# The weight sums of the Strassen groups as accumulating DMAs, each group in two items

## The chip, the cores and the metric

One core of one Trainium2 chip runs the kernel. The metric is the time of one execution in microseconds (us) on the device. Two runs of the kernel before took 727.15 and 727.75 us, median 727.45.

The engines are named as in the profile: PE (TensorE's matmuls), PEld (its weight loads), DVE (VectorE), ACT (ScalarE), POOL (GpSimd) and SP (SyncE, which here only issues DMAs).

## What is computed

One decoder layer on 256 tokens of width 1024 in float32: a SwiGLU feed-forward part, a mixing part (a state-space branch and a differential-attention branch, merged by gates), and a second SwiGLU feed-forward part, each between two RMS norms and with a residual. The edited code stands in the two feed-forward parts:

```python
def swiglu(x, w_gate, w_up, w_down):
    return (jax.nn.silu(x @ w_gate) * (x @ w_up)) @ w_down
...
h = h + 0.5 * rmsnorm(swiglu(rmsnorm(h, ffn1_pre_g[l]), ffn1_w_gate[l], ffn1_w_up[l], ffn1_w_down[l]),
                      ffn1_post_g[l])
...
h = h + 0.5 * rmsnorm(swiglu(rmsnorm(h, ffn2_pre_g[l]), ffn2_w_gate[l], ffn2_w_up[l], ffn2_w_down[l]),
                      ffn2_post_g[l])
```

`w_down` is 2816 x 1024: 11 row blocks of 256.

## The kernel before

**Weights.** All weights come through one list, `chunks`, of 1 MB pieces in the order of use. SP loads them (L164) into raw tiles `raw<i>`: three buffers with the tag "raw", and for a few chunks (`IN_U8`) one of two buffers with the tag "u8" that the normed activations leave free meanwhile. `load_next` issues the next load when a chunk's last reader has been written down; on the chip, the load waits until its buffer is free.

**Splits.** PE multiplies in float32r. Each operand is split into a high part, a cast on ACT (L258), and the rest, a subtraction on DVE (L259); a product is made of three matmuls (high x high, low x high, high x low). A split of half a chunk, 128 x 1024 elements, is one *step*: one cast, one subtraction, two tiles from the pool of 28 "k4" buffers. `split_to` writes steps down some way ahead of the product that needs them (`AHEAD`, `STEPS`). ACT, DVE, PE and SP execute in the order written; POOL's order is left to the framework's scheduler. A step therefore waits for its raw tile, for the step before it on ACT and DVE, and for PE to have finished with the k4 buffers that it reuses.

**The down projection.** `mm_n` (L489) multiplies the 256 tokens (two blocks of 128) with the row blocks of `w_down`, in the order of the table `DOWNS`. A plain row block (`0`, `1`, ...) is one chunk: two steps and 24 matmuls of 128 x 512. A pair such as `(2, 3)` is a *group*: its 512 rows, its 256 tokens and its 1024 columns are halved, and the 2 x 2 x 2 block product is done in 7 products instead of 8, the Strassen-Winograd form. `quarters` (L655) forms and splits the activations' quarters and their sums; `piece_steps` (L191) those of the weights. The weights of a group are two chunks, whose column halves are named b11 and b12 (first chunk) and b21 and b22 (second). Their sums are formed in place, by four subtractions on DVE (L209) between the seven splits; `piece` (L520) issues the seven products, 6 matmuls each. Three of them gather in PSUM tiles of their own over all groups of a part (`acc_m`: m5, m6, m7) and one in m1; after the last group `sums_of` and `sum_up` (L529, L535) add them to the four accumulators `acc_f`.

In the first part two groups, in the second three, all of them among plain blocks. The last `TAIL` (3; in the second part 2) plain blocks are multiplied at the end, one accumulator after the other, so that the norm behind them (`post_norm`) starts early. The gain row of that norm, `pg_f`, is loaded by POOL (L486).

Of the kernel before, what the change touches and what calls it, by code (L numbers as in the profile page):

```python
# [24 lines left out]
P = 128  # L25
T = 256
# [17 lines left out]
DOWNS = (((2, 3), 0, (4, 5), 1, 6, 7, 8, 9, 10), ((2, 3), 0, (4, 5), 1, 8, (6, 7), 9, 10))  # L44
# [7 lines left out]
def tile_hybrid_layer(ctx: ExitStack, tc: tile.TileContext, x, ffn1_pre_g, ffn1_w_gate, ffn1_w_up,  # L52
# [37 lines left out]
    chunks, pieces, in_u8 = [], set(), set()  # L90

    def t_chunk(w, k0, c0):
        chunks.append((w[k0:k0 + D, c0:c0 + T].rearrange("(j p) c -> p j c", p=P), [P, KD, T]))

    def s_chunk(w, k0, c0):
        chunks.append((w[k0:k0 + 512, c0:c0 + 512].rearrange("(j p) c -> p j c", p=P), [P, 4, 512]))

    def n_chunk(w, k0):
        chunks.append((w[k0:k0 + 2 * P, :].rearrange("(j p) c -> p j c", p=P), [P, 2, D]))

    w_in2 = w_in[0]
    Z0, XS0, B0, C0, DT0, Q0, KK0, V0, G0 = 0, 2048, 4096, 4608, 5120, 5152, 6176, 7200, 8224

    def ffn_chunks(wg, wu, wd, downs, first=False):
# [5 lines left out]
        n = 0  # L110
        for item in downs:
            if isinstance(item, tuple):
                pieces.add(len(chunks))
                n += 1
                in_u8.update(len(chunks) + m for m in range(2) if (not first, n, m) in IN_U8)
            for j in item if isinstance(item, tuple) else (item,):
                n_chunk(wd[0], j * T)
# [30 lines left out]
    def load_next(i):  # L148
        n = i + 1 + RAW_BUFS
        while n - len(in_u8.intersection(range(i + 1, n))) < i + 1 + RAW_BUFS:  # L150
            n += 1
        load_to(n)

    def load_to(n, at={}):
        while len(raws) < min(n, len(chunks)):
            i = len(raws)
            src, shape = chunks[i]
            if i in in_u8:
                r = sb.tile(shape, F32, tag="u8", name=f"raw{i}", bufs=2)
            else:  # L160
                r = sb.tile(shape, F32, tag="raw", name=f"raw{i}", bufs=RAW_BUFS)
# [6 lines left out]
    def split_steps(ahead=True):  # L168


        i = len(splits)
        load_to(i + 1)
# [4 lines left out]
        for q in range(2):  # L177
# [5 lines left out]
            for j in range(0, nj, n):  # L183
                js = slice(j, j + n)
                f = split(hi[:, js, :], lo[:, js, :], r[:, q * nj + j:q * nj + j + n, :])
                if i in behind:
                    tc.add_manual_dep(f.ins, behind[i], order, reason="behind the sums")
                if (q, j + n) == (1, nj):
                    raws[i] = r = None
                    if ahead:  # L190
                        load_next(i)  # L191
                yield

    def piece_steps():


        i = len(splits)
        load_to(i + 2)
        (b11, b12), (b21, b22) = ([r[:, :, q * 512:(q + 1) * 512] for q in range(2)] for r in raws[i:i + 2])
        pairs = []  # L200
        splits.extend((pairs, None))
        sums = {0: (b11, b12, b11), 1: (b12, b22, b12), 4: (b22, b22, b11), 5: (b21, b21, b22)}
        for n, out in enumerate((b11, b21, b22, b11, b12, b22, b21)):
            hi = k4([P, 2, 512], f"shi{i}{n}", F32R)
            lo = k4([P, 2, 512], f"slo{i}{n}", F32R)
            split(hi, lo, out)
            pairs.append((hi, lo))
            if n in sums:
                nc.vector.tensor_tensor(*sums[n], ALU.subtract)  # L209
            if n > 4:  # L210
                raws[i + n - 5] = None
                load_next(i + n - 5)
# [4 lines left out]
    def advance():  # L217

        while True:
            if under[0] is None:  # L220
                if len(splits) == len(chunks):
                    return False
                steps_at.extend([made_steps[0]] * (len(splits) + 1 - len(steps_at)))
                under[0] = piece_steps() if len(splits) in pieces else split_steps()
# [5 lines left out]
    def split_to(n, steps=0):  # L230

        while len(splits) < min(n, len(chunks)):
# [6 lines left out]
    def take(ahead=AHEAD):  # L239
# [6 lines left out]
        nj = chunks[i][1][1] // 2  # L246
        return (lambda j: his[j // nj][:, j % nj, :], lambda j: los[j // nj][:, j % nj, :])

    def take_part(n):
# [3 lines left out]
        if n == 6:  # L253
            taken[0] += 2
# [68 lines left out]
    halves = (slice(0, 512), slice(512, D))  # L323
# [165 lines left out]
    def mm_n(acc, acts, ready, turned, begun=lambda: None, items=(0, 1, 2, 3), tail=TAIL):  # L489
# [3 lines left out]
        held, sums = [], [None]  # L493
# [23 lines left out]
        def piece(c):  # L517
            outs = ((m1, 1), (acc[0][0], (0, 0)), (acc[0][1], (0, 1)), (m5, 5), (m7, 7), (m6, 6),
                    (acc[1][0], (1, 0)))
            for n, (out, key) in enumerate(outs):  # L520
                wh, wl = take_part(n)
                for kt in range(2):
                    ah, al = acts[c][n][kt]
                    for x_, w_ in ((ah, wh), (al, wh), (ah, wl)):
                        product(key, out, x_, w_[:, kt, :], kt == 1 and w_ is wl and c == inner[-1])
            del acts[c]

        def add(out, in_, x_):
            return nc.vector.tensor_tensor(out, in_, x_, ALU.add)  # L529

        def sums_of():
# [4 lines left out]
            for out, in_, x_, at in ((u2, m6, u1, None), (u4, m5, u2, (0, 1)), (u2, m7, u2, (1, 0)),  # L536
                                     (u3, m5, u2, (1, 1))):
                add(out, in_, x_)
# [3 lines left out]
        def sum_up(b, q):  # L542
            f = add(acc[b][q], acc[b][q], sums[0].pop((b, q)))
# [7 lines left out]
        for c in items[:-tail]:  # L551
            if isinstance(c, tuple):
                piece(c)
                if c == inner[-1]:
                    sums_of()
                continue
# [89 lines left out]
    def ffn(post_v, tag, products, ready, turned, then):  # L646
# [9 lines left out]
        def quarters(j0, j1):  # L656
# [15 lines left out]
            for n in range(2):  # L672
                split(fh[:, 2 * n:2 * n + 2], fl[:, 2 * n:2 * n + 2], f[n])
            acts[(j0, j1)] = [[(h_[:, n, k, :], l_[:, n, k, :]) for k in range(2)]
                              for h_, l_, n in ((ah, al, 0), (ah, al, 1), (fh, fl, 3), (fh, fl, 0), (fh, fl, 2),
                                                (fh, fl, 1), (ah, al, 2))]
# [68 lines left out]
    def first_products(evict, back):  # L745
# [33 lines left out]
        def ends(c):  # L779
            raws[c] = None  # L780
            load_to(c + 1 + RAW_BUFS)
# [679 lines left out]
```

## Time and profile before

| what | value |
|---|---|
| median of 2 runs | 727.45 us |
| the profiled execution | 727.35 us |
| its span in the trace | 725.6 us |
| granted clock of TensorE | 0.998 |
| DVE busy | 559.6 us, 77% of the span |
| ACT busy | 435.6 us, 60% |
| groups of the first part on PE | 130.3 to about 155 us |
| groups of the second part on PE | 663.7 to 673.2, 678.7 to 688.2, 699.1 to 708.6 us |

How to read it: the span runs from the first to the last instruction of the trace. A row of the list of groups has the line, the engine, the operation and the tiles (numbers left out), then the count, the busy time and the mean in ns, then the idle time of the engine before them and what ended it. A row of the chain has start, length and what ran. A row of the list of waits has the waiting instruction, the one waited for, the total in us, how often, and the longest. "raw<-raw" at L209 are the in-place sums of weights; "shi" and "slo" the split tiles of a group, "whi" and "wlo" those of a plain chunk.

### The profile page before, as it was taken

The page shows a single profiled execution, that of the slowest core. Times are in us where ns is not written, and L with a number is a line of the kernel's source. Part 1 is how long each engine was busy: PE and PEld are TensorE (multiplying, and loading weights), DVE is VectorE, ACT ScalarE, POOL GpSimd, SP SyncE. Part 2 cuts the span into 40 slices and gives each one's busy share as a digit, 9 for nine tenths or more (in the row PEclk, how much of TensorE's full clock was granted, in tenths as well). Part 3 has the DMA queues.
Part 4 walks back from the last instruction along what each step waited for, and adds up shares of the span by engine and source line. Part 5 has one row for each costly group of instructions (what it writes and reads, how often), then busy time and mean ns, then how long its engine had stood idle before and what let it go on. Part 6 is the DMA issues. An engine that isn't in the chain of part 4 may idle for free.

```text
span 725.6 us, 12188 instructions
## 1 busy us (share of the span) xinstructions
PE 716.9 (99%) x4917; PEld 652.9 (90%) x4917; DVE 559.6 (77%) x814; ACT 435.6 (60%) x703; POOL 34.7 (5%) x74
## 2 busy tenths in 40 slices
PE   8999999999999999999999999999999999999996
PEld 7899999888889999999998888888888999999885
DVE  5858769897668889876978988696684875578985
ACT  6735535665557565977966465974563645456642
POOL 0800000000300000000000000000010000000000
PEclk9999999999999999999999999999999999999999
DMA  8976364758453558565656655375361755765611
GB/s 320 286 221 220 129 232 146 289 175 285 128 174 117 188 164 272 166 205 189 216 163 190 210 192 175 116 244 191 118 230 60 231 184 168 231 231 193 227 76 58
DMA packets 94216, 138.03 MB, mean 190 GB/s; under 512 B 2684, under 2 KB 68304, under 8 KB 94160
## 3 DMA queue, kind: packets, MB, share of 16 engines
q1 hardware_dynamic: 91488, 129.51, 53.7%
q0 software_dynamic: 2368, 7.22, 3.3%
q8 instruction: 38, 0.62, 0.3%
q10 hardware_dynamic: 304, 0.53, 0.2%
q14 instruction: 18, 0.15, 0.1%
HBM read 136.17 MB, written 1.08 MB: 189 GB/s over the span
## 4 chain that ended last, share of the span: by engine, by line
PE 98%; ACT 1%; DMA 1%; DVE 0%; issue 0%; DVEq 0%; SPq 0%
PE acc_f L498 12%; PE pgt L283 6%; PE pws L283 6%; PE pg_f L268 5%; PE pg_f L269 5%; PE pup_f L269 4%; PE pup_f L268 4%; PE pup_f L271 4%; PE pg_f L271 4%; PE acc_m L498 4%; PE pn_f L776 3%; PE pn_mx L283 3%; PE pn_f L283 3%; PE acc_mx L498 3%; PE pwd L283 3%; PE pxs L268 2%
## 5 line engine op out<-in xcount | busy, mean ns | idle before, releaser
L259 DVE TENSOR_TENSOR wlo<-raw,whi 128x1024 fp32r<-128x1024 f32 (+1 forms) x226 | 265.8, 1211 | 27.3 <-ACT whi L258 23.5
L258 ACT CAST whi<-raw 128x1024 fp32r<-128x1024 f32 (+1 forms) x226 | 224.6, 1041 | 42.5 <-DMA raw<-in_ffn_w_up_dram 18.9
L269 PE MATMUL pg_f<-u_f,whi 128*128 128x256 f32 x288 | 67.1, 276 | 0.0
L269 PE MATMUL pup_f<-u_f,whi 128*128 128x256 f32 x288 | 67.1, 276 | 0.0
L268 PE MATMUL pg_f<-u_f,whi 128*128 128x256 f32 x288 | 67.1, 276 | 0.0
L268 PE MATMUL pup_f<-u_f,whi 128*128 128x256 f32 x288 | 67.0, 276 | 0.0
L268 PEld LDWEIGHTS pg_f<-u_f,whi 128*128 128x128 f32 x288 | 54.1, 188 | 0.0
L269 PEld LDWEIGHTS pup_f<-u_f,whi 128*128 128x128 f32 x288 | 54.1, 188 | 0.0
L268 PEld LDWEIGHTS pup_f<-u_f,whi 128*128 128x128 f32 x288 | 54.1, 188 | 0.0
L269 PEld LDWEIGHTS pg_f<-u_f,whi 128*128 128x128 f32 x288 | 54.0, 188 | 0.0
L258 ACT CAST shi<-raw 128x1024 fp32r<-128x1024 f32 x35 | 35.8, 1052 | 29.2 <-DVE raw L209 16.1
L259 DVE TENSOR_TENSOR slo<-raw,shi 128x1024 fp32r<-128x1024 f32 x35 | 42.1, 1219 | 2.2 <-PE acc_m L498 1.4
L271 PE MATMUL pup_f<-u_f,wlo 128*128 128x256 f32 x288 | 38.5, 276 | 0.0
L271 PE MATMUL pg_f<-u_f,wlo 128*128 128x256 f32 x288 | 38.5, 276 | 0.0
L721 DVE TENSOR_TENSOR sg_f<-pup_f,sg_f 128x512 f32<-128x512 f32 x18 | 12.4, 688 | 32.3 <-PE pup_f L271 32.3
L271 PEld LDWEIGHTS pg_f<-u_f,wlo 128*128 128x128 f32 x288 | 35.3, 188 | 0.0
L271 PEld LDWEIGHTS pup_f<-u_f,wlo 128*128 128x128 f32 x288 | 35.3, 188 | 0.0
L498 PE MATMUL acc_f<-whi,gh_f 128*128 128x512 f32 x96 | 33.5, 390 | 0.0
L498 PE MATMUL acc_f<-whi,gl_f 128*128 128x512 f32 x96 | 33.5, 389 | 0.0
L498 PE MATMUL acc_f<-wlo,gh_f 128*128 128x512 f32 x96 | 33.5, 389 | 0.0
L283 PE MATMUL pgt<-whi,u_mx 128*128 128x512 f32 x128 | 33.0, 394 | 0.0
L268 PE MATMUL pxs<-u_mx,whi 128*128 128x256 f32 x128 | 30.3, 280 | 0.0
(376 smaller groups left out, 1659.5 us busy)
## 6 DMA issues: line engine op xcount, KB each, us to landing
raw<-in_w_in_dram SPq DMA_DIRECT2D x40, 1024.0 KB, 5.4
raw<-in_ffn_w_down_dram SPq DMA_DIRECT2D x22, 1024.0 KB, 5.9
raw<-in_ffn_w_gate_dram SPq DMA_DIRECT2D x20, 1024.0 KB, 6.3
raw<-in_ffn_w_up_dram SPq DMA_DIRECT2D x20, 1024.0 KB, 5.6
raw<-in_ssd_w_branch_dram SPq DMA_DIRECT2D x8, 1024.0 KB, 5.1
acb<-acd POOLq DMA_DIRECT2D x8, 512.0 KB, 4.5
raw<-in_da_w_branch_dram SPq DMA_DIRECT2D x4, 1024.0 KB, 5.3
raw<-in_w_out_dram SPq DMA_DIRECT2D x4, 1024.0 KB, 5.1
```

The costliest lines, as they stand in the source:

```text
L258: nc.scalar.copy(hi, src)
L259: return nc.vector.tensor_sub(lo, src, hi.bitcast(F32))
L268: nc.tensor.matmul(acc[m], wh(j)[:, cs], ah(k0 + j), start=first and j == ks[0], stop=False)
L269: nc.tensor.matmul(acc[m], wh(j)[:, cs], al(k0 + j), start=False, stop=False)
L271: i = nc.tensor.matmul(acc[m], wl(j)[:, cs], ah(k0 + j), start=False, stop=last and j == ks[-1])
L283: nc.tensor.matmul(acc, a(k0 + j), b(j), start=first and i == 0, stop=last and i == 11)
L498: nc.tensor.matmul(out, a, w, start=key not in begun_at, stop=last, skip_group_check=bool(inner))
L721: nc.vector.tensor_tensor(sg, pu_, sg, ALU.mult)
L776: nc.tensor.matmul(acc[b][i], s, m, start=q == 0 and j == 0 and e == 0, stop=q == 1 and j == 3 and e == 2)
```

## The change

The four DVE subtractions of each group become five DMAs from GpSimd that add their source to their destination in SBUF (`accum_op=ALU.add`). [...] Four of the DMAs read another quarter of the group's raw tiles, one reads b12 again from HBM.

Each group becomes two items in `DOWNS`, with the plain block that followed the group between them (in the second part block 8 moves into the third group for this). The first item splits b11, b21 and b22 and makes three products; as each is split, an add makes of that quarter the sum that the second item needs. The second item splits b12, b11, b22 and b21, now all sums, makes the other four products, and only then gives the two raw tiles back.

```diff
-DOWNS = (((2, 3), 0, (4, 5), 1, 6, 7, 8, 9, 10), ((2, 3), 0, (4, 5), 1, 8, (6, 7), 9, 10))
+DOWNS = (((2, 3), 0, (2, 3), (4, 5), 1, (4, 5), 6, 7, 8, 9, 10), ((2, 3), 0, (2, 3), (4, 5), 1, (4, 5), (6, 7), 8, (6, 7), 9, 10))
...
+    def add_on(out, in_):
+        nc.gpsimd.dma_start(out, in_, accum_op=ALU.add)
+
     def piece_steps():
...
-        (b11, b12), (b21, b22) = ([r[:, :, q * 512:(q + 1) * 512] for q in range(2)] for r in raws[i:i + 2])
+        part, i = units[len(splits)]
+        (b11, b12), (b21, b22) = ([quarter(i, k, q) for q in range(2)] for k in range(2))
         pairs = []
-        splits.extend((pairs, None))
-        sums = {0: (b11, b12, b11), 1: (b12, b22, b12), 4: (b22, b22, b11), 5: (b21, b21, b22)}
-        for n, out in enumerate((b11, b21, b22, b11, b12, b22, b21)):
...
+        splits.append(pairs)
+        if part is item_a:
+            add_on(b12, b22)
+        for n, out in enumerate((b11, b21, b22) if part is item_a else (b12, b11, b22, b21)):
...
             split(hi, lo, out)
             pairs.append((hi, lo))
-            if n in sums:
-                nc.vector.tensor_tensor(*sums[n], ALU.subtract)
-            if n > 4:
-                raws[i + n - 5] = None
-                load_next(i + n - 5)
+            if part is item_a:
+                if n == 0:
+                    add_on(b11, chunks[i][0][:, :, halves[1]])
+                elif n == 1:
+                    add_on(b21, b22)
+                else:
+                    add_on(b22, b11)
+                    add_on(b21, b11)
+            elif n in (1, 3):
+                free_raw(i + n // 2)
             yield
...
-        def piece(c):
-            outs = ((m1, 1), (acc[0][0], (0, 0)), (acc[0][1], (0, 1)), (m5, 5), (m7, 7), (m6, 6),
-                    (acc[1][0], (1, 0)))
+        def piece(c, part):
+            outs = ((m1, 1), (acc[0][0], (0, 0)), (acc[0][1], (0, 1))) if part == 0 else \
+                ((m7, 7), (m5, 5), (m6, 6), (acc[1][0], (1, 0)))
...
-            nc.vector.tensor_tensor(f1, a21, a22, ALU.add)
+            nc.vector.tensor_tensor(f1, a22, a21, ALU.subtract)
             nc.vector.tensor_tensor(f3, a11, a21, ALU.subtract)
-            nc.vector.tensor_tensor(f2, f1, a11, ALU.subtract)
+            nc.vector.tensor_tensor(f2, f1, a11, ALU.add)
```

Loads follow the buffers: `load_next` is replaced by `free_raw`, which issues the next load of the list when a buffer of its tag is free.

On DVE, the group (4, 5) of the second feed-forward part (its chunks are raw114 and raw115; raw116 is the plain chunk of block 1). Before:

```order
L259 TENSOR_TENSOR slo1140_7322<-raw114_7277,shi1140_7321 128x1024
L259 TENSOR_TENSOR slo1141_7333<-raw115_7289,shi1141_7332 128x1024
L209 TENSOR_TENSOR raw114_7277<-raw114_7277 128x2x512
L259 TENSOR_TENSOR slo1142_7344<-raw115_7289,shi1142_7343 128x1024
L209 TENSOR_TENSOR raw114_7277<-raw115_7289,raw114_7277 128x2x512
L259 TENSOR_TENSOR slo1143_7348<-raw114_7277,shi1143_7347 128x1024
L209 TENSOR_TENSOR raw115_7289<-raw115_7289,raw114_7277 128x2x512
L259 TENSOR_TENSOR slo1144_7376<-raw114_7277,shi1144_7375 128x1024
L209 TENSOR_TENSOR raw115_7289<-raw115_7289 128x2x512
L259 TENSOR_TENSOR slo1145_7387<-raw115_7289,shi1145_7386 128x1024
L259 TENSOR_TENSOR slo1146_7402<-raw115_7289,shi1146_7401 128x1024
L259 TENSOR_TENSOR wlo1160_7412<-raw116_7291,whi1160_7411 128x1024
```

And in the changed program:

```order
L286 TENSOR_TENSOR slo1140True_7340<-raw114_7270,shi1140True_7339 128x1024
L286 TENSOR_TENSOR slo1141True_7351<-raw115_7272,shi1141True_7350 128x1024
L286 TENSOR_TENSOR slo1142True_7362<-raw115_7272,shi1142True_7361 128x1024
L286 TENSOR_TENSOR wlo1160_7374<-raw116_7294,whi1160_7373 128x1024
L286 TENSOR_TENSOR wlo1161_7384<-raw116_7294,whi1161_7383 128x1024
L286 TENSOR_TENSOR slo1140False_7396<-raw114_7270,shi1140False_7395 128x1024
L286 TENSOR_TENSOR slo1141False_7406<-raw114_7270,shi1141False_7405 128x1024
L286 TENSOR_TENSOR slo1142False_7418<-raw115_7272,shi1142False_7417 128x1024
L286 TENSOR_TENSOR slo1143False_7422<-raw115_7272,shi1143False_7421 128x1024
```

The four sums (L209) are gone, and the last four splits stand behind the two of the plain chunk.

On POOL, from the start of the second part's groups to the end of the program. Before there is one DMA:

```order
L440 TENSOR_SCALAR dr_f2_5993<-ident_89,r_f20_5832 128x128
L486 DMA pg_f2_7251<-in_ffn2_post_g_dram 128x1024
```

In the changed program:

```order
L466 TENSOR_SCALAR dr_f2_5995<-ident_89,r_f20_5834 128x128
L214 DMA raw111_6946<-in_ffn2_w_down_dram 128x2x512
L214 DMA raw111_6946<-raw112_7009 128x2x512
L214 DMA raw112_7009<-raw112_7009 128x2x512
L512 DMA pg_f2_7256<-in_ffn2_post_g_dram 128x1024
L214 DMA raw112_7009<-raw111_6946 128x2x512 x2
L214 DMA raw114_7270<-raw115_7272 128x2x512
L214 DMA raw114_7270<-in_ffn2_w_down_dram 128x2x512
L214 DMA raw115_7272<-raw115_7272 128x2x512
L214 DMA raw115_7272<-raw114_7270 128x2x512 x2
```

Five adds a group stand in POOL's queue (the third group's five follow in the same way). The last two of a group wait for the landing of its first three; the gain row of the norm stands among those of the first group.

More of the change, by code (lines that the diff above doesn't have):

```diff
@@ L110, in ffn_chunks @@
         n = 0
+        at = {}
         for item in downs:
-            if isinstance(item, tuple):
-                pieces.add(len(chunks))
+            if not isinstance(item, tuple):
+                n_chunk(wd[0], item * T)
+            elif item in at:
+                units.append((item_b, at[item]))
+            else:
+                at[item] = len(chunks)
                 n += 1
                 in_u8.update(len(chunks) + m for m in range(2) if (not first, n, m) in IN_U8)
-            for j in item if isinstance(item, tuple) else (item,):
-                n_chunk(wd[0], j * T)
+                units.append((item_a, len(chunks)))
+                for j in item:
+                    n_chunk(wd[0], j * T, False)
     ffn_chunks(ffn1_w_gate, ffn1_w_up, ffn1_w_down, DOWNS[0], True)
@@ L146, in tile_hybrid_layer, with tag_of, free_raw @@
     taken = [0]
[L148 to L152, printed above, removed]
+    live = {"raw": 0, "u8": 0}
+    def tag_of(i):
+        return ("u8", 2) if i in in_u8 else ("raw", RAW_BUFS)
+    def free_raw(i):
+        raws[i] = None
+        live[tag_of(i)[0]] -= 1
+        while len(raws) < len(chunks) and live[tag_of(len(raws))[0]] < tag_of(len(raws))[1]:
+            load_to(len(raws) + 1)
     def load_to(n, at={}):
@@ L157, in load_to @@
             src, shape = chunks[i]
[L158 to L161, printed above, removed]
+            tag, n_bufs = tag_of(i)
+            live[tag] += 1
+            r = sb.tile(shape, F32, tag=tag, name=f"raw{i}", bufs=n_bufs)
             nj = shape[1] // 4 if i == 0 else shape[1] // 2 if i < 4 else shape[1]
@@ L220, in advance @@
             if under[0] is None:
[L221 removed]
+                if len(splits) == len(units):
                     return False
                 steps_at.extend([made_steps[0]] * (len(splits) + 1 - len(steps_at)))
[L224 removed]
+                under[0] = split_steps() if units[len(splits)][0] is None else piece_steps()
             if next(under[0], STOP) is not STOP:
@@ L230, in split_to @@
     def split_to(n, steps=0):
-        while len(splits) < min(n, len(chunks)):
+        while len(splits) < min(n, len(units)):
             if not advance():
@@ L492, in mm_n @@
         plain = [c for c in items if not isinstance(c, tuple)]
-        held, sums = [], [None]
+        held, sums, halved = [], [None], set()
         begun_at, open_ = set(), {(b, q) for b in range(2) for q in range(2)}
@@ L535, in sums_of @@
             nc.scalar.copy(u1, m1)
-            for out, in_, x_, at in ((u2, m6, u1, None), (u4, m5, u2, (0, 1)), (u2, m7, u2, (1, 0)),
+            for out, in_, x_, at in ((u2, u1, m6, None), (u4, m5, u2, (0, 1)), (u2, m7, u2, (1, 0)),
                                      (u3, m5, u2, (1, 1))):
-                add(out, in_, x_)
+                add(out, in_, x_, ALU.add if at else ALU.subtract)
                 if at and c == items[-tail - 1]:
@@ L542, in sum_up @@
         def sum_up(b, q):
-            f = add(acc[b][q], acc[b][q], sums[0].pop((b, q)))
+            f = add(acc[b][q], acc[b][q], sums[0].pop((b, q)), ALU.subtract if q else ALU.add)
             if not sums[0]:
```

65 lines of the change are left out of this document (36 added, 29 removed).

## The prediction

> **What bounds the kernel now.** I read the page's first and fourth parts, then the waits of PE, then the two stretches in which the edited code runs.
>
> ```profile
> span 725.6 us, 12188 instructions
> PE 716.9 (99%) x4917; PEld 652.9 (90%) x4917; DVE 559.6 (77%) x814; ACT 435.6 (60%) x703; POOL 34.7 (5%) x74
> PE 98%; ACT 1%; DMA 1%; DVE 0%; issue 0%; DVEq 0%; SPq 0%
> ```
>
> ```profile
> PE warm L350 <- POOL ident L334: 1.6, 1, 1.6
> PE pwd L283 <- ACT o L1229: 0.5, 1, 0.5
> PE pu_f L755 <- DVE u_f L764: 0.3, 1, 0.3
> PE pn_f L776 <- ACT u_f L762: 0.2, 1, 0.2
> ```
>
> TensorE is busy for 716.9 of 725.6 us, the chain that ended last is 98% PE, and all PE waits together are 1.6 + 0.5 + 0.3 + 0.2 = 2.6 us, none of them at a Strassen product. So nothing done on DVE, ACT or a queue can win more than 2.6 us unless it also removes matmuls. The two stretches of the groups (down projections of the first and the second feed-forward part):
>
> ```profile
> core 0: us, PE busy (x) PEld busy (x) DVE busy (x) ACT busy (x) POOL busy (x), PEclk, DMA share, GB/s
> 130.20:183.50 53.30, 53.30 (x237) 44.11 (x237) 48.48 (x51) 33.78 (x40) 0.88 (x2) 1.00 0.75 267
> 663.70:719.40 55.70, 55.70 (x246) 45.80 (x245) 47.98 (x51) 27.97 (x35) 0.00 (x0) 1.00 0.43 159
> ```
>
> PE is full in both, at a granted clock of 1.00. DVE is the next engine (48.5 of 53.3 us), but it keeps ahead. What PE wants, and when, in the second part:
>
> ```profile
> 663.67 1.38 PE acc_m L498 x6
> 665.05 2.72 PE acc_f L498 x12
> 667.77 4.08 PE acc_m L498 x18
> 671.85 6.80 PE acc_f L498 x30
> ...
> 707.21 12.25 PE acc_f L498 x54
> ```
>
> A product is 6 matmuls, 1.36 us; a plain chunk 24 matmuls, 5.44 us (6.80 less one product). Seven products and a chunk are 15.0 us.
>
> **The change, part by part.** *Matmuls:* 7 products a group stay 7, with the same 42 matmuls; the first three now go ahead of the neighbouring plain chunk and the last four behind it. On PE: nothing. *DVE:* the four in-place sums of weights of each of 5 groups go:
>
> ```profile
> L209 DVE TENSOR_TENSOR raw<-raw x10: 1215/1218/1225, 116.7 to 697.0; 128x1024 f32<-128x1024 f32 x10
> L209 DVE TENSOR_TENSOR raw<-raw,raw x10: 1216/1218/1225, 117.9 to 694.7; 128x1024 f32<-128x1024 f32 x10
> ```
>
> That is 20 x 1.218 = 24.4 us off DVE, and worth 0 on the path, since PE waited for none of them; the cover that they had (PE's products) stays. The changed signs in the activations' sums and in the sums of products are one instruction for one, at no cost. *GpSimd:* 25 accumulating DMAs of 512 KB come in, five a group, with a chain inside. With A1..A3 the splits of the first item, P1, P2 those of the plain chunk, B1..B4 those of the second: once A1 is split, b11 takes in b12 from HBM; once A2 is split, b21 takes in b22; once A3 is split and the earlier adds have landed, b22 and then b21 take in b11. B1 and B2 wait for one add, B3 and B4 for two in a row. They stand in ACT's and DVE's program order, so behind a late B3 or B4 wait the next group's A1, and in the last group the splits of the last two chunks. That is the new risk. GpSimd's queue has one foreign member among them, the gain row pg_f2, which goes out when PE lets its buffer go:
>
> ```profile
> 656.28 0.63 POOL L486 DMA_DIRECT2D pg_f<-in_ffn_post_g_dram  x1 [108.97 <-PE pg_f L269]
> ```
>
> It holds up only the first group's two last adds, and those are issuable later than this anyway (660.9, below).
>
> *SyncE:* a group's two raw tiles are held through the second item, so loads that follow start later. In the second part the tile after group (2,3) waits for that group's B2 split and last adds (669.2, below) instead of a split at about 660; at 6.3 us it lands at 675.5, and PE wants it at 682.7. The tile behind it waits for B4 (671.5) and lands by 671.5 + 9.3 = 680.8, ten us before its cast. Both stay hidden, so 0; what it costs if not is in the last part.
>
> *How long an add takes* the trace does not show. The nearest rows:
>
> ```profile
> pg_f<-in_ffn_post_g_dram POOLq DMA_DIRECT2D x2, 512.0 KB, 3.8
> acd<-acT POOLq DMA_DIRECT2D x1, 32.0 KB, 1.8
> ```
>
> and, for the 1024 KB loads of weights from 639 to 705 us,
>
> ```profile
> DMA to landing us min/median/max: 4.9/6.3/9.3
> ```
>
> Below, an add costs as much as a plain GpSimd transfer of its bytes, 3.8 us. Above, an add reads two operands, 1024 KB, and meets the loads on the same DMA engines: 9.3 us, the slowest load. I take W = 6.3, the median of 1024 KB in this stretch, and 3.8 - 1.8 = 2.0 us more for the second of two adds issued together. The Trainium skill, page "DMA: Bandwidth & Descriptors", section "Anatomy of one DMA — SWDGE (gpsimd) path", fits a plain GpSimd DMA as 2.0 us plus bytes over 436 GB/s. By it 512 KB take 3.2 us (the trace has 3.8), and an estimate for two operands is 4.4 us, under which everything below would be hidden and the time 727.4.
>
> *The chain in the second part*, at W = 6.3. A split is a cast of 1.05 and a subtraction of 1.22 us, 2.3 together:
>
> ```profile
> L259 DVE TENSOR_TENSOR slo<-raw,shi 128x1024 fp32r<-128x1024 f32 x15 | 18.2, 1220 | 2.2 <-PE acc_m L498 1.4 <-ACT shi L258 0.6
> L258 ACT CAST shi<-raw 128x1024 fp32r<-128x1024 f32 x14 | 14.4, 1050 | 14.5 <-DVE raw L209 10.3 <-DMA raw<-in_ffn_w_down_dram 3.0 <-PE acc_f L498 1.2
> ```
>
> Group (2,3): its second weight tile lands at 652.26 (ACT waits for the DMA until then).
>
> ```profile
> 652.26 2.96 ACT L258 CAST shi<-raw 128x1024 fp32r<-128x1024 f32 x3 [3.77 <-DMA raw<-in_ffn_w_down_dram]
> ```
>
> A2 is split at 654.6; its add lands at 660.9; b22's second add at 667.2, b21's at 669.2; B4's cast ends at 670.25. PE wants B4 at 663.67 + 4.08 + 5.44 + 4.08 = 677.27: hidden.
> Group (4,5) queues behind it: the casts of A1 and A2 end at 671.3 and 672.35, A2's subtraction at 673.6; adds land at 679.9, 686.2 and 688.2; B3 is split at 688.5 (PE: 690.87), B4 at 690.5 (PE: 692.23): hidden, by 2 us.
> Group (6,7): A2's subtraction ends at 692.6; adds land at 698.9, 705.2, 707.2. B3's cast ends at 706.25 and its subtraction at 707.5. PE is at B3 at 705.83 and needs the low half two matmuls (0.46 us) later: 1.2 us late. B4's low half comes at 709.5, wanted at 708.9: 0.6 more. Behind B4 stand the four splits of the last two chunks, which before were long done:
>
> ```profile
> 700.52 4.63 DVE L259 TENSOR_TENSOR wlo<-raw,whi 128x1024 fp32r<-128x1024 f32 x4
> 707.32 0.69 DVE L529 TENSOR_TENSOR u_(6, 7)_7594<-acc_m,u_(6, 7)_7593 128x512 f32<-128x512 f32 x1 [2.17 <-PE acc_m L498]
> ```
>
> One each 1.16 us, the last at 714.2, while PE takes one each 0.68 us (half a chunk's columns, 3 matmuls) and would want the last at 712.8: 1.4 more. In all 1.2 + 0.6 + 1.4 = 3.2 us. W enters four times in a row (two chains of two, the second begun behind the first), so the loss is about 4 x (W - 5.5), and 0 below 5.5.
>
> *The first part* has two groups and more room:
>
> ```profile
> 145.45 1.36 PE acc_m L498 x6
> ```
>
> ```profile
> 137.99 2.35 DVE L259 TENSOR_TENSOR slo<-raw,shi 128x1024 fp32r<-128x1024 f32 x2
> ```
>
> Group (4,5) begins on PE at 145.45, its B4 at 145.45 + 4.08 + 5.44 + 4.08 = 159.05. Its A2 is split by 140.3, so B4 by 140.3 + 2W + 2.0 + 2.3 = 157.2, and it is late only for W over 7.4, by 2 x (W - 7.4). At 6.3: 0.
>
> Sum: the profiled execution took 727.35 us (its span 725.6 and 1.75 around it), 0.1 from the median of 727.45. 727.35 + 0 (PE) + 0 (DVE) + 3.2 = 730.5.
>
> **The rivals.** *All hidden* (W up to 5.5): 727.4. For it: 3.8 us for the same bytes of one operand. Against it: two operands, and loads landing at 6.3.
> *Slower: the adds crawl beside the loads.* Place: B3 and B4 of the last groups. Extra = 4 x (W - 5.5) + 2 x (W - 7.4), which passes 14.5 us (2%) at W = 8.6. At W = 9.3 it is 15.2 + 3.8 = 19.0, so 746.4. For it: the DMA engines are 0.75 and 0.43 busy in the two stretches and a load took up to 9.3. Against it: the last group's adds meet only the last loads. The Trainium skill's page "DMA: Bandwidth & Descriptors", section "Issuing engines are not separate DMA queues", says that DMAs of all engines run on the same 16 DMA engines and interleave; by that rule this rival gains, and the spread of 4.9 to 9.3 between equal loads agrees with it.
> *Faster.* DVE's 24.4 us could matter only where PE waits for DVE: 2.6 us of waits at the most, 724.8; over 2% is out of reach without fewer matmuls.
> *The change does not do what it says:* the adds are so spread by the queue that each B item is simply served a little later but in time, nothing moves at all, 727.4.
>
> **How the numbers follow.** Forecast, W from 5.5 to 8.6, loss 0 to 14.5, 730.5 at the middle W: 0.42. Hidden: 0.34. Slow adds, over 2%: 0.20. Faster by over 2%: 0.01. Undone: 0.03. A difference of 2% is about what a measurement of this kernel can tell from none. Within 2% are 0.42 + 0.34 + 0.03 = 0.79; slower 0.20; faster 0.01. The forecast's own range is 727.4 to 742. The range for 8 in 10 goes from 726.5 (a third of the 2.6 us of waits gone) to 745 (W of 9.1), which leaves out most of the slow case and little else.
>
> **What would show it.** Right: PE busy time unchanged near 716.9; L209 gone from DVE; new rows of 512 KB adds on GpSimd's queue landing in 5 to 8 us; ACT's shi casts waiting for these DMAs; a PE wait of 1 to 5 us in total at acc_m and acc_f in the last group, and little in the first part. Hidden: PE's waits stay at 2.6 us and the adds land under 5.5. Wrong: adds of 9 us and more with PE waits in both parts; or PE waits at products of A items, which would mean that late loads of weights (their buffers are held through the second item), and not the chain of adds, set the time; or a longer start or end with PE's waits unchanged.

## The result and the profile after

The changed kernel takes 771.9 us (two executions, 770.16 and 773.64) against 727.45 before: 1.061 times the time, 95% interval 1.051 to 1.072, slower. The forecast was 730.5 us with a range up to 745. The profiled execution is the one of 773.64 us.

The page's first part and its chain, in the form shown for before:

```profile
span 771.9 us, 12254 instructions
PE 735.3 (95%) x4917; PEld 660.1 (86%) x4917; DVE 537.7 (70%) x794; ACT 435.2 (56%) x703; POOL 64.3 (8%) x99
PE 74%; DMA 15%; issue 4%; DVE 3%; ACT 2%; POOL 1%; SPq 0%; DVEq 0%; POOLq 0%; ACTq 0%
```

DVE lost its sums (559.6 to 537.7 us) as the change says. PE has the same 4917 matmuls, yet is busy for 18.4 us longer and idle for 36.6 us (8.7 before). 15% of the chain that ended last is now DMA. The waits of PE say whose:

```profile
PE acc_m L524 <- ACT shi1142False L285: 8.4, 1, 8.4
PE acc_m L524 <- ACT shi252False L285: 5.2, 1, 5.2
PE acc_m L524 <- ACT shi1172False L285: 4.0, 1, 4.0
PE acc_f L524 <- DVE acc_f L556: 3.6, 2, 2.0
PE acc_m L524 <- ACT shi251False L285: 2.4, 1, 2.4
```

`shi1142False` is the high half of the split of b22 in the second item (False) of the group whose first weight tile is 114: tile numbers 22 and 25 are groups (2,3) and (4,5) of the first part, 111, 114 and 117 are (2,3), (4,5) and (6,7) of the second. All large waits but one are at B2 and B3, the splits behind adds; none is at a first item or for a weight load. The other, 3.6 us for `acc_f`, is for the sums of products at the end of each part (2.0 and 1.6), which DVE makes behind the late splits. The two stretches of the groups, from the first product of the first group to the end of the part (columns as before):

```profile
134.55:206.00 71.45, 60.39 (x235) 46.45 (x235) 44.34 (x47) 34.44 (x42) 7.03 (x8) 0.88 0.88 260
686.10:771.90 85.80, 63.46 (x248) 47.33 (x246) 41.49 (x46) 28.89 (x40) 14.45 (x12) 0.89 0.73 183
```

Before, the first took 53.2 us (130.2 to 183.4) and the second, with the end of the kernel, 62.2 (663.4 to 725.6). So 18.3 us were lost in the first part and 23.6 in the second. The stretch between the parts is the same (480.0 us). The other 4.4 us lie ahead of the first group, in code that is unchanged: over the profiled executions of this case, that first product comes at 130.1 to 131.4 us in nine (before among them) and at 133.9 to 134.6 in five, whatever the edit, so these 4.4 are not the change's. 4.4 + 18.3 + 23.6 = 46.3 = 771.9 - 725.6.

How long DMAs took from issue to landing (median):

```profile
raw<-in_ffn_w_down_dram SPq DMA_DIRECT2D x22, 1024.0 KB, 7.4
raw<-raw POOLq DMA_DIRECT2D x20, 512.0 KB, 7.5
...
pg_f<-in_ffn_post_g_dram POOLq DMA_DIRECT2D x2, 512.0 KB, 12.6
```

The median add takes 7.5 us, not 6.3, and the row of the gain, 3.8 us before and the lower of the two bounds between which W was taken, is now 12.6. The chain that ended last shows how adds and splits hang together in the second part, from the add of group (2,3) behind A2 to the last landing of group (6,7):

```profile
677.99 7.92 DMA raw<-raw
...
685.97 0.49 issue
686.47 0.43 POOL raw L214
...
687.20 11.49 DMA raw<-raw
...
698.77 1.06 ACT shi1113False L285
...
702.52 1.13 POOL raw L214
703.65 14.44 DMA raw<-raw
...
731.61 7.50 DMA raw<-raw
...
740.25 0.73 POOL raw L214
740.98 7.13 DMA raw<-raw
```

Read downward: an add lands (677.99 + 7.92 = 685.91); half a microsecond later GpSimd issues the pair behind it, one after the other, 0.73 us apart; the second lands at 698.69; only then ACT casts B4 (`shi1113False`), and only behind that, in ACT's own order, the next group's A1. The next group's add goes out at 703.65. The profile's chain leaves out the landing of that group's pair (it follows GpSimd's queue there); the second add of this pair went out at 719.38, landed at 726.63, and B4 and the next group's A1 came behind it on ACT:

```profile
726.74 1.04 ACT L285 CAST shi1143False<-raw 128x1024 fp32r<-128x1024 f32 x1 [1.76 <-DMA raw<-raw]
```

So six landings stand in a row.

### The profile page after: what moved, and what is told of

It reads as the page before. It is cut to its first block, busy times and chain, and to the rows that moved or that the text cites. A ratio compares the mean times of both kernels' runs of the same rounds, so it can differ in the third digit from the quotient of the medians.

```text
span 771.9 us, 12254 instructions
## 1 busy us (share of the span) xinstructions
PE 735.3 (95%) x4917; PEld 660.1 (86%) x4917; DVE 537.7 (70%) x794; ACT 435.2 (56%) x703; POOL 64.3 (8%) x99
## 3 DMA queue, kind: packets, MB, share of 16 engines
q0 software_dynamic: 9168, 20.33, 12.9%
## 4 chain that ended last, share of the span: by engine, by line
PE 74%; DMA 15%; issue 4%; DVE 3%; ACT 2%; POOL 1%; SPq 0%; DVEq 0%; POOLq 0%; ACTq 0%
DMA raw<-raw 12%; PE pgt L310 6%; PE pws L310 6%; PE acc_f L524 3%; PE pup_f L298 3%; PE pg_f L296 3%; PE pup_f L296 3%; PE pg_f L295 3%; PE pg_f L298 3%; PE pup_f L295 3%; PE pn_mx L310 3%; PE pn_f L310 3%; PE acc_mx L524 3%; PE pn_f L804 3%; PE pwd L310 3%
## 5 line engine op out<-in xcount | busy, mean ns | idle before, releaser
L295 PE MATMUL pg_f<-u_f,whi 128*128 128x256 f32 x288 | 68.3, 279 | 0.0
L295 PE MATMUL pup_f<-u_f,whi 128*128 128x256 f32 x288 | 68.3, 278 | 0.0
L296 PE MATMUL pg_f<-u_f,whi 128*128 128x256 f32 x288 | 68.3, 279 | 0.0
L296 PE MATMUL pup_f<-u_f,whi 128*128 128x256 f32 x288 | 68.3, 278 | 0.0
L749 DVE TENSOR_TENSOR sg_f<-pup_f,sg_f 128x512 f32<-128x512 f32 x18 | 12.4, 688 | 34.2 <-PE pup_f L298 34.2
L214 POOL DMA_DIRECT2D raw<-raw x20 | 24.5, 1388 | 73.2 <-DMA raw<-raw 42.5
L295 PE MATMUL pz<-u_mx,whi 128*128 128x256 f32 x128 | 30.3, 280 | 0.0
```

Of the source, the lines that this page charges most:

```text
L214: nc.gpsimd.dma_start(out, in_, accum_op=ALU.add)
L295: nc.tensor.matmul(acc[m], wh(j)[:, cs], ah(k0 + j), start=first and j == ks[0], stop=False)
L296: nc.tensor.matmul(acc[m], wh(j)[:, cs], al(k0 + j), start=False, stop=False)
L749: nc.vector.tensor_tensor(sg, pu_, sg, ALU.mult)
```

## The experiments

The first theory had three parts: adds are slow because they share the DMA engines with weight loads; those landings, six in a row behind one another in the order of ACT and DVE, are the loss; and the lower clock after PE's waits adds to it. Rivals: an add is slow by its own form; the two items and the later release of raw tiles are the cause, whoever makes the sums; the adds' traffic does it by delaying loads, whoever waits for them. "First" and "second" below are the losses of the two stretches against before, read as above. A time without an interval is that of one execution.

**All sums on DVE, the rest of the change kept.**

```diff
-        nc.gpsimd.dma_start(out, in_, accum_op=ALU.add)
+        nc.vector.tensor_tensor(out, out, in_, ALU.add)
```

> The changed kernel with its two items, its signs and its later release of raw tiles, but each of the 25 sums of weights made by a DVE instruction in place of a GpSimd DMA (b11 takes in b12 first, b12 takes in b22 after it, so that no second read of b12 is needed). Theory (the adds land late, 10 to 16 us where 6.3 were assumed, because they share the DMA engines with the weight loads; everything else in the change is harmless): PE waits near the 2.6 us of before, both stages of the groups back to 53 and 56 us, 727 to 730 us; DVE gets 25 x 1.22 = 30.5 us of sums where before had 24.4, so up to 3 us may be lost where DVE is full. Rival (the split into two items itself holds the raw buffers longer, and loads come late): PE waits of 10 us and more stay, 755 us or over.

Measured: 727.77 us, ratio to before 0.9998 (0.9975 to 1.0021); PE's waits are those of before, both losses 0.0. Two items, the later release and the signs that moved from the weights' sums to the activations' sums and the sums of products cost nothing. The adds as DMAs are the whole loss. DVE's 5.5 us more than before (565.1 busy) were hidden.

**Adds by themselves.** The loop of phases is all that runs:

```diff
+        for k, l_ in enumerate(ls):
+            nc.sync.dma_start(l_, block(k))
+            ...
+                nc.gpsimd.dma_start(x_[:, :, hs], in_, accum_op=ALU.add)
```

> Only DMAs: all of the layer's computation is left out, and a tile is stored as the output. Four repeats of phases that start together after a DVE instruction: one GpSimd copy of 512 KB between SBUF tiles, one accumulating copy (an add), a pair of adds, a copy and an add with an HBM source, one and three 1 MB loads, an add beside 1, 2, 3 and 6 loads that start with it, a copy beside 3 and 6, a pair beside 3, and the same sum by DVE. Theory (contention): an add alone 5 us, the second of a pair 7, growing with the loads that are in flight: about 7 beside one, 10 or more beside three, 13 to 16 beside six; the loads are slowed as well. Rival (the add is slow by its own form): 8 us or more alone, little more beside loads.

Its time says nothing; the rows of DMA issues do (median us to landing at the end):

```profile
loads_ld<-in_ffn_w_down_dram SPq DMA_DIRECT2D x12, 1024.0 KB, 7.0
add_three_ld<-in_ffn_w_down_dram SPq DMA_DIRECT2D x12, 1024.0 KB, 10.0
...
copy<-source POOLq DMA_DIRECT2D x4, 512.0 KB, 3.2
add<-source POOLq DMA_DIRECT2D x4, 512.0 KB, 5.0
...
add_one<-source POOLq DMA_DIRECT2D x4, 512.0 KB, 7.4
add_two<-source POOLq DMA_DIRECT2D x4, 512.0 KB, 10.7
add_three<-source POOLq DMA_DIRECT2D x4, 512.0 KB, 12.4
add_six<-source POOLq DMA_DIRECT2D x4, 512.0 KB, 12.4
copy_three<-source POOLq DMA_DIRECT2D x4, 512.0 KB, 8.6
```

Contention: 5.0 us alone, where the rival (slow by its own form) had 8 or more, and 7.4, 10.7 and 12.4 beside one, two and three loads. Beside six it stays at 12.4, where 13 to 16 were expected. Three loads are slowed by one add from 7.0 to 10.0.

**No loads of plain chunks in the second part** (wrong weights in these products).

```diff
+UNLOADED = {113, 116, 119, 120, 121}
...
+            if i in UNLOADED:
+                raws.append(h)
+                continue
```

> The changed kernel, with the five plain chunks of down weights in the second feed-forward part (5 loads of 1 MB) not loaded: their splits read the residual tile instead, so these products are of wrong weights; as many splits and matmuls as before. The first part is untouched and serves as control. Theory (contention): the adds of the second part land in 5 to 6 us (7 to 8 for the second of a pair) instead of 8 to 14, the part's stage shrinks from 79.7 us to 56 to 62, the first part stays at 71.6, and the time is 748 to 755. Rival (an accumulating DMA of this form takes 8 to 14 us by itself, or the adds delay one another): the second stage stays at 75 to 80 us and the time at 766 to 773.

Measured: 760.5 us; first 16.7, second 16.4. Neither theory's number. The first part was left as it is in the changed kernel and lost 16.7 where it had lost 18.3, so a microsecond or two between single executions says little. Without these loads most adds of the second part did land in 5 to 8 us, and still 16.4 of 23.6 us were lost. So loads are a part of it, and a row of six landings, five of them of 7.1 to 7.8 us and one of 12.1, is already too long.

**The same in both parts**, a missing load holding its place among the buffers.

```diff
+UNLOADED = {24, *range(27, 33), 113, 116, 119, 120, 121}
...
             live[tag] += 1
+            if i in UNLOADED:
+                raws.append(h)
+                continue
```

> The changed kernel without the loads of the plain down chunks in both parts (7 in the first, 5 in the second; their splits read the residual tile, so these products are of wrong weights); a missing load holds its place among the three raw buffers, so that all other loads go out as in the changed kernel. The run that left them out in the second part alone won 7 of the 24 us that this part lost; the rest stayed with adds at 5 to 9 us. If loads do the same in both parts: first stage 62 to 67 us (71.5 in the changed kernel, 53.2 before), time 750 to 758. If contention with plain loads is the cause in the first part, where the DMA engines are fuller (0.84 against 0.76): first stage 54 to 58, time 742 to 748. If it matters in neither: 765 or more.

Measured: 760.8 us; first 13.0, second 16.4. The first stage took 66.2 us, where 62 to 67 were expected if loads do the same in both parts; the time is almost 3 us over, and this execution has the 4 us ahead of the first group.

**Matmuls of zeros in PE's waits.**

```diff
+                for _ in range(FILL.get((i, n), 0) if part else 0):
+                    product(key, out, zero_r, prev[:, 0, :])
```

> The changed kernel with 80 added matmuls with a stationary of zeros (8 and 22 ahead of the second and third product of the first part's group (4,5), 2 and 32 in the second part's, 16 ahead of the third of group (6,7)), 0.23 us each, which fill the waits that PE had there and add zero to the sums. Theory (after a wait TensorE is granted a lower clock, and the 18.4 us by which PE's busy time grew are paid on the path as far as the next wait does not swallow them): matmuls stay 0.23 us apart, time 756 to 764. Rival (the lower clock only fills time in which PE would wait for the next add anyway): 768 to 773, with longer waits in its place.

Measured: 770.9 us; first 20.1, second 23.7. The second stretch, with 50 of the 80 added matmuls:

```profile
683.20:769.20 86.00, 71.87 (x299) 54.33 (x297) 41.47 (x46) 28.97 (x40) 13.65 (x12) 0.98 0.73 182
```

The granted clock is back at 0.98 (0.98 in the first as well) and nothing is won, 43.8 us lost in the two stretches against 41.9: this part of the theory falls. PE's slow stretches lie in time in which it would otherwise have waited for the next landing.

**Plain copies in place of adds** (sums not formed).

```diff
-        nc.gpsimd.dma_start(out, in_, accum_op=ALU.add)
+        nc.gpsimd.dma_start(out, in_)
```

> The changed kernel with its 25 GpSimd DMAs made plain copies of the same tiles, in the same places and with the same waits (the sums of weights are not formed, so the products are of wrong weights). In the kernel of DMAs alone a copy landed in 3.2 us alone and 8.6 beside three loads, where an add took 5.0 and 12.4. Theory (the groups' stages are set by chains of six landings in a row, so what counts is how long one landing takes): the six landings fall from about 58 us to about 40, PE waits to under 8 us, and the time is 728 to 738. Rival (not the length of a landing, but GpSimd's issue, the waits for DMAs and the later release of tiles cost the time): 755 us or more.

Measured: 739.7 us, 1.7 over the theory's upper end and far from the rival; first 6.6, second 5.5. As many DMAs, bytes, issues and waits, but each lands sooner: about 70% of the loss is gone.

**Copies, and no loads of plain chunks.**

```diff
+UNLOADED = {24, *range(27, 33), 113, 116, 119, 120, 121}
...
-        nc.gpsimd.dma_start(out, in_, accum_op=ALU.add)
+        nc.gpsimd.dma_start(out, in_)
```

> The changed kernel with its 25 adds made plain copies and without the loads of the plain chunks of both parts (wrong weights in both), all waits in place. With copies alone the two stages lost 6.6 and 5.5 us, without the loads alone 13.0 and 16.4, as the changed kernel 18.3 and 23.7. Theory (what a stage loses follows from how long the landings in its chain take): copies land in 3 to 5 us, both stages lose under 3 us, 727 to 733 us. Rival (half of what copies lost is GpSimd's issue and the order of the queues, whatever the landings): each stage still loses 4 us or more, 735 us or more.

Measured: 728.9 us beside 728.7 for before; first 0.8, second -0.2. Every GpSimd DMA of the change, and every wait for one, is still there. Only the plain chunks' loads are missing and the landings shorter, and the loss is gone.

These runs fit one line. For the second part, the six landings of the chain (in each group the add behind A2, then the second of the pair), read from the trace DMA by DMA:

| kernel | the six landings, us | sum S | second lost | S less the loss |
|---|---|---|---|---|
| zeros in waits | 8.2 11.7 15.6 7.3 7.4 7.2 | 57.4 | 23.7 | 33.7 |
| the changed kernel | 7.9 11.5 14.4 7.3 7.5 7.1 | 55.7 | 23.6 | 32.1 |
| next group first | 7.4 11.5 14.4 7.3 7.4 7.1 | 55.1 | 24.1 | 31.0 |
| no plain loads, both | 7.8 12.3 7.2 7.1 7.3 7.1 | 48.8 | 16.4 | 32.4 |
| no plain loads | 7.8 12.1 7.1 7.1 7.3 7.1 | 48.5 | 16.4 | 32.1 |
| copies | 3.9 10.6 10.5 4.0 4.4 5.1 | 38.5 | 5.5 | 33.0 |
| copies, no plain loads | 3.8 5.6 7.0 4.0 4.5 4.0 | 28.9 | -0.2 | (hidden) |

The part loses S - 32.3 us, within 1.4, once S is over that. The line was read off these runs afterwards, and they are three kinds of run (S near 56, 49 and 39), not six; "next group first" is described below and differs in the first part alone.

**The second level of sums on DVE**, one landing in a row for each group.

```diff
-                    add_on(b22, b11)
-                    add_on(b21, b11)
+                    nc.vector.tensor_tensor(b22, b22, b11, ALU.add)
+                    nc.vector.tensor_tensor(b21, b21, b11, ALU.add)
```

> The changed kernel with the two sums that come second in a group's chain (b22 takes in b11, b21 takes in b11) made by DVE, 1.2 us each; the three first ones stay GpSimd adds. One landing in a row for each group in place of two. Theory (chain): a group's chain goes from about 20 us to about 15 (2.3 for a split, 1.1 for a second issue, 7 to 10 for the landing, 2.4 of DVE, 2.3 for a split), which is the 15.0 us that PE takes for a group and a chunk, so the loss is 0 to 10 us: 728 to 738. Rival (contention alone: the first adds land in 10 to 16 us beside the loads whatever follows them): 745 us or more.

Measured: 751.9 us; first 9.5, second 11.1. Missed by 14 us; it is the rival's number, and in the groups (4,5) the rival's landings too (10.0 to 15.2 us for the first adds, 5.9 to 8.5 in the other groups). DVE's waits in the two parts:

```profile
DVE raw L236 <- DMA raw<-raw: 14.7, 2, 9.3
```

```profile
DVE raw L236 <- DMA raw<-raw: 19.6, 3, 10.8
```

The sums now wait on DVE for the first adds, and behind them stand the splits of plain chunks that were free of adds before. The wait was moved to another queue; how much of the loss that is, and how much the long landings, this run does not separate.

**The first level on DVE, the second as adds** (10 adds, no DVE sum waits for a DMA).

```diff
-                    add_on(b21, b22)
+                    nc.vector.tensor_tensor(b21, b21, b22, ALU.add)
```

(and the sums of b11 and b12 likewise)

> The changed kernel with the three first sums of a group (b11 takes in b12, b12 takes in b22, b21 takes in b22) made by DVE, and the last two (b22 and b21 take in b11) left as GpSimd adds: 10 adds in place of 25, one landing in a row for each group, and no DVE instruction waits for a DMA except the splits of the third and fourth tile of a second item. Theory (what the second part loses is the sum of the landings in a row, six of them, less about 34.5 us; with three landings of 7 to 12 us and 1.2 us of DVE in place of each other one the sum stays under that): 727 to 733 us, adds landing in 5 to 9 us, PE waits under 6 us. Rival (adds beside weight loads are harmful however few stand in a row): 740 us or more.

Measured: 741.6 us, 1.019 times before (1.015 to 1.023); first 3.4, second 9.2. Over the theory's number, and in the rival's range (740 or more). The three landings left in the second part's row (12.9, 9.5 and 7.3 us) sum to 29.7, under 32.3, and yet 9.2 us were lost: the line for six landings does not hold for this chain. It leaves out that all three sums also stand ahead of the next splits on DVE; that this is the difference is argued, not shown. ACT still waits for the adds at B3 of each group, most at that of group (4,5):

```profile
ACT shi1142False L284 <- DMA raw<-raw: 10.1, 1, 10.1
```

**The next group's first item ahead of the second item**, in the first part only.

```diff
-DOWNS = (((2, 3), 0, (2, 3), (4, 5), 1, (4, 5), 6,
+DOWNS = (((2, 3), (4, 5), 0, (2, 3), 1, (4, 5), 6,
```

> The changed kernel with one other order in the first part: the first item of group (4,5) goes ahead of chunk 0 and of the second item of group (2,3), so its splits and adds no longer queue on ACT and DVE behind the late last splits of group (2,3). As many instructions and DMAs as in the changed kernel; the second part is untouched. Theory (the chains follow one another because a group's first split stands behind the other group's last one in program order): both chains overlap, PE wants the last sums of group (4,5) some 11 us later beside the start of its chain, first stage 53 to 58 us in place of 71.5, time 750 to 757. Rival (queueing matters little, the adds are late by themselves and overlapping ones slow each other): first stage 66 us or more, time 764 or more.

Measured: 769.0 us; first 16.0 (69.2 us), second 24.1. Missed: 53 to 58 was expected for the first stretch, and both numbers are the rival's. The chain in this stretch:

```profile
130.46 10.91 DMA raw<-in_ffn_w_down_dram
144.24 10.55 DMA raw<-raw
156.07 14.63 DMA raw<-raw
```

The second weight tile of group (4,5) lands at 141.4, since its load (10.9 us) meets the first group's pair. So the add behind A2 goes out 12.8 us after PE's first product (131.43), only 3.5 us sooner than in the changed kernel. Its own last pair, alone in the changed kernel (7.1 us), now meets the loads of plain chunks and takes 14.6. Queueing in program order was thus not isolated by this run.

**Adds that nothing computes with** (sums on DVE). Three kernels were needed. In the first the spare adds read the split tiles:

```diff
+        nc.gpsimd.dma_start(dumps[n_spare[0] % 2], src.bitcast(F32), accum_op=ALU.add)
```

> The kernel with all sums of weights on DVE (727.8 us) and beside them 25 GpSimd adds of 512 KB from the split tiles into two spare tiles, issued at the same places as the adds of the changed kernel, five a group, which nothing computes with and nothing but a reused buffer waits for; 26 in place of 28 split buffers make room for the spare tiles. Theory (the time is lost in waits for landings, not by the traffic): the adds land in 5 to 15 us and the weight loads beside them in up to 12, but both are hidden, 727 to 733 us. Rival (the traffic itself delays the weight loads so that PE waits for them): 740 us or more, with PE waits for splits of plain chunks whose casts wait for loads.

Measured: 767.1 us, 1.055 times before (1.051 to 1.060): the rival's number, but not its reason. The waits of ACT and of DVE:

```profile
ACT shi1170True L299 <- DMA dump<-slo1141True: 9.5, 1, 9.5
```

```profile
DVE slo1113False L300 <- DMA dump<-shi1112True: 9.5, 1, 9.5
```

A split waited to write a buffer that a spare add was still reading. The test was faulty; it shows that a slow DMA also holds what it reads.

The second set each add off by a one-column GpSimd copy, and read HBM:

```diff
+        nc.vector.tensor_copy(g_, src[:, 1, 511:512].bitcast(F32))
+        nc.gpsimd.tensor_copy(dumps[n][:, 0, 0:1], g_)
+        nc.gpsimd.dma_start(dumps[n], chunks[22][0][:, :, halves[n]], accum_op=ALU.add)
```

> As the run before it (all sums of weights on DVE, 25 GpSimd adds of 512 KB beside them), with its fault mended: there the adds read the split buffers and held them until they landed, so ACT and DVE waited for 9 us at a time to write the next split. Now an add reads weights from HBM into one of two spare tiles, and is set off by a copy of one column on DVE behind the same split, so that no split, product or raw buffer waits for it. Theory (the time goes in waits for landings): 727 to 733 us, although the adds and the loads beside them land late. Rival (the traffic of the adds delays the weight loads that PE needs): 738 us or more, with the idle time of ACT's casts ended by weight loads.

Measured: 758.6 us, 1.039 (1.034 to 1.043), the rival's number. Again not its reason alone: PE's last product ends 19.6 us before the end of the span (6.2 before), since the kernel's end waits for spare adds that had fallen late. From the second part's first product to its last it is only 2.0 us more than before (58.0 and 56.0). The first part lost 9.6 us, 5.4 of them in one wait of PE for the norm behind the part.

```profile
SPq L1501 <- DMA dump<-in_ffn_w_down_dram: 14.0, 1, 14.0
```

The third sets them off directly behind the same splits, into spare arrays in HBM:

```diff
+        d = nc.gpsimd.dma_start(dumps[n // 5 * 2 + n % 5 % 2], src, accum_op=ALU.add)
+        tc.add_manual_dep(d.ins, f.ins.name, mybir.DependencyInfo(mybir.DependencyClass.Sync,
+                                                                  mybir.DependencyReason.DATA), reason="behind the split")
```

> All sums of weights on DVE (727.8 us) and beside them the same 25 adds of 512 KB by GpSimd, set off directly by the same splits as in the changed kernel, from the residual tile (or, as there, one in five from the weights in HBM) into spare arrays in HBM, so that no split buffer, raw tile, GpSimd instruction or spare tile stands between them and the work, and no add falls behind into the end of the kernel as in the run before. Theory (most of the loss is waits for landings; traffic alone costs what the run before showed between its first product and its last, 2 us in the second part, and 4 to 10 in the first): 729 to 739 us. Rival (traffic alone makes most of the loss): 745 us or more, with PE idle at products whose weights land late.

Measured: 739.12 us, 1.0163 (1.0146 to 1.018), at the upper end of the theory's range; first 5.0, second 6.1. Loads and adds land as late as in the changed kernel (7.4 and 7.5 us) or later, and ACT waits for loads, here in the second part:

```profile
raw<-in_ffn_w_down_dram SPq DMA_DIRECT2D x22, 1024.0 KB, 8.6
...
dump<-h POOLq DMA_DIRECT2D x20, 512.0 KB, 8.1
```

```profile
ACT whi L300 <- DMA raw<-in_ffn_w_down_dram: 12.4, 3, 6.7
```

So the traffic alone, by late loads, makes 11 us here. If that share carries over to the changed kernel, the waits of splits for landings make the other 31 of its 42 us; this is a difference, not a measurement of its own. And these adds write HBM, those of the changed kernel SBUF.

## Why the prediction was wrong, step by step

**The bound, PE, DVE: right.** Nothing was to be won (the kernel with sums on DVE takes the same time as before), and DVE's sums went without effect. PE's busy time did grow, by its clock; that step ("On PE: nothing") holds for the time all the same, by the run with zeros.

**"W = 6.3": the term that failed first.** An add alone takes 5.0 us, and the second of a pair 7.1 in the trace where nothing else runs (740.98): both lie under the 6.3 and the 8.3 that the sum used. But the row that W was taken from, loads of 1 MB, was measured in a stretch without adds. 25 adds bring their own traffic, and meet the loads: the six landings of the second part took 7.1 to 14.4 us, and came to 55.7 us where the sum had 3 x (6.3 + 8.3) = 43.8. That is 11.9 us of the 20.4 by which the part was missed (23.6 - 3.2).

**The chain around the landings: the rest, 8.5 us.** The sum let an add start when the one before it lands. The trace has 0.5 us from a landing to GpSimd's next issue, and 0.7 to 1.1 us between two issues: about 5 us over the six. PE was a microsecond nearer to group (2,3). And from the last landing to the end of the span it took 23.8 us (748.1 to 771.9) where the sum had 21.6 (707.2 to 728.8): the splits behind the last B4 took the 7 us forecast, but the sums of products stand behind them on DVE, and PE waits for these sums. The part loses nothing only up to S = 32.3, which is W = 4.4, not 5.5.

**"4 x (W - 5.5)": wrong slope.** The forecast's own working put the casts of group (4,5) behind B4 of (2,3), so that group's two landings are in the row as well: six, not four. At the forecast's own W the measured line gives 43.8 - 32.3 = 11.5 us for this part, where 3.2 were forecast.

**The first part, "0".** Three things failed. The forecast took A2 of group (4,5) as split at 140.3, as in before, and counted that group's two landings alone. But here too its A1 stands on ACT behind B4 of group (2,3), so that the changed kernel's chain has that group's landings in it as well:

```profile
132.42 13.54 DMA raw<-raw
145.98 1.06 ACT shi223False L285
...
150.85 15.66 DMA raw<-raw
167.80 7.09 DMA raw<-raw
```

Then, its second weight tile, loaded beside the pair and the gain row, landed 12.7 us after its issue, at 146.24, and would have held A2 nearly as long without that queue. By both, the add behind A2 went out 16.3 us after PE's first product (150.85) and not 10.1 as in before. And the landings of group (4,5) were 15.7 and 7.1 us, 8.2 more than 6.3 + 8.3. 8.2 + 6.2 - 1.9 of reserve make 12.5 of the 18.3 us; 2.0 more are PE's wait for the sums of products at the part's end, ahead of which the chain has a plain chunk's load issued only at 179.51; the rest is not traced.

**"Both stay hidden, so 0" for late loads** was right for their being released later (sums on DVE: no loss), wrong for their sharing the engines with adds (spare adds: 11 us).

**The rivals.** "The adds crawl beside the loads" was the right one, in place and mechanism, and had 0.20; its size was too small, 746.4 us at W = 9.3, since it used the same slope. It was given too little: "the last group's adds meet only the last loads" was true of the last group alone, and the other two set the chain.

## What to carry to other kernels

A DMA in place of an instruction trades busy time of an engine for the time of a landing; where work behind it stands in program order, add up the landings in a row and compare the sum with what the bounding engine needs for that stretch, before looking at any engine's share. Take the length of a landing with the new transfers counted in: here a row measured without them was too short (5.0 us alone, 12.4 beside three loads). An idle-looking resource (DVE had room, the DMA engines 0.43 to 0.75 busy) did not say here whether the chain fits.

## What the runs showed of the hardware

**An accumulating DMA costs the DMA engines about twice a copy.** GpSimd's queue in the changed kernel, and with copies:

```profile
q0 software_dynamic: 9168, 20.33, 12.9%
```

```profile
q0 software_dynamic: 5968, 20.33, 8.1%
```

For the same bytes, 128 more packets an add. Less the 3.3% of before, an add takes (0.129 x 771.9 - 0.033 x 725.6) / 25 = 3.0 us of all 16 engines, a copy (0.081 x 738.0 - 0.033 x 725.6) / 25 = 1.4.

**A slow clock need not be paid.** After a wait of 5.2 us, matmuls of 512 columns start 0.43 us apart, later again 0.23:

```profile
175.55 0.63 PE L524 MATMUL acc_m<-shi252False,qfl_f 128*128 128x512 f32 x1
175.98 0.63 PE L524 MATMUL acc_m<-slo252False,qfh_f 128*128 128x512 f32 x1
...
185.13 0.39 PE L524 MATMUL acc_f<-whi,gh_f 128*128 128x512 f32 x1
185.36 0.39 PE L524 MATMUL acc_f<-whi,gl_f 128*128 128x512 f32 x1
```

The Trainium skill, page "TensorE: Matmul & The Clock Gate", section "HAM oscillation — how this bites in real kernels", describes this drop behind waits for DMAs and counts the slow matmuls' excess as extra time. The drop agrees with these rows; the price does not show here: PE's busy time grew by 18.4 us, and keeping the clock up won nothing (43.8 us lost in the two stretches against 41.9).

**DVE can hold GpSimd up for 10 us.** In the second kernel with spare adds, a GpSimd copy of one column (median 0.59 us) took 10.17 us while DVE ran ten splits without a gap (the last four in the second row); GpSimd's spans in the trace are rough. The rows of GpSimd and of DVE:

```profile
716.63 10.17 POOL L226 COPY dump<-go 128x1 f32<-128x1 f32 x1 [3.28 <-DVE wlo L304]
```

```profile
722.14 4.62 DVE L304 TENSOR_TENSOR wlo<-raw,whi 128x1024 fp32r<-128x1024 f32 x4
```

The Trainium skill, page "SBUF — State Buffer", section "SBUF: two separate sides", has a lock on a port pair between a GpSimd instruction that reads SBUF and a DVE instruction with two SBUF inputs; this row agrees. An add was not slowed in the one row looked at: without plain loads, one issued amid such DVE work (splits without a gap from 694.36 to 702.40) landed in 7.13 us, as the second of a pair does alone:

```profile
698.15 7.13 DMA raw<-raw
```
